# Wider VectorE operations, more raw slots, a third early granule pair and a spread residual in four feed-forward networks

## The chip, the core and the metric

One Trainium2 chip, one of its cores. The time is that of one execution of the whole program in device microseconds; the figure to compare is the median of several executions. One further execution was taken by the hardware profiler, and all rows below are from that one.

## What is computed

The input is 256 tokens of width 1024 and a conditioning vector c. A first block of two layers is followed by a second block of one layer with attention and a mixture of experts. Each of the two layers of the first block does, with nine columns sh, sc, g that are cut from `silu(c) @ w_ada[l] + b_ada[l]` (a vector of 9 x 1024):

```python
h = rmsnorm(x, norm_g[l, 0]) * (1 + sc1) + sh1
x = x + 0.5 * g1 * ((silu(h @ wg0) * (h @ wu0)) @ wd0)
h = rmsnorm(x, norm_g[l, 1]) * (1 + sc2) + sh2
x = x + g2 * mixer(h)            # l = 0: attention and pooling; l = 1: short convolution
h = rmsnorm(x, norm_g[l, 2]) * (1 + sc3) + sh3
x = x + 0.5 * g3 * ((silu(h @ wg1) * (h @ wu1)) @ wd1)
```

So there are four feed-forward networks, each 1024 to 2816 to 1024, all in float32. The change concerns these four, and what they share with the rest.

## The kernel before, in words

**Arithmetic.** Every float32 operand of a large product is split into a part that is rounded to the matmul's input format (ScalarE cast, line 227) and a remainder (VectorE subtraction, line 228). A product then is high x high + high x low + low x high. `mm2` (lines 238 to 243) does this with two matmuls: the weight's high part against both halves of the activation (512 columns), and the weight's low part against the high half (256 columns). `mm3`, and `pair` (lines 128 to 141), use three of 256 columns. Activations are held transposed: partition = feature, 256 tokens along the free dimension.

**A feed-forward network** is `ffn` (line 440). The 2816 inner features are eleven granules p = 0 to 10 of 256. For each granule one 1 MB tile of gate weights and one of up weights is loaded and split, two halves f of 128 features are accumulated in PSUM (f = 0: gate, up; f = 1: gate, up), and the result silu(gate) x up is split into an activation tile. Then comes the down projection in two halves h = 0, 1 of 512 output features. Each half runs over six pairs of granules (the last pair has one granule), with one 1 MB weight tile per pair; four accumulators live through the half, and after it the residual is added (line 526), squares are summed for the next norm, and the next norm's operand is built (`gap_chunk`, line 97).

**Granules that do not need h.** The norm's scale per token is known late. In the second to fourth network, granules 0 and 1 therefore multiply the weights with the merely scaled x (`aH`, `aL` in the tile xa); scale per token and shift are applied to the result (`gap_pair`, line 104; `gap_fin`, line 143). During granule 1 the eight chunks of the true h are built by GpSimd, ScalarE and VectorE (`h_chunk`, line 405, last step line 417), and granules 2 to 10 use h. In the first network granule 0 runs on h while the first columns are still being computed (`first_cols`), and granules 1 to 10 follow.

**Columns of w_ada.** 15 of the 18 column vectors are computed beside the networks and mixers. `gemv_steps` (line 295) is a generator; each step loads one 1 MB tile and does two VectorE operations of 1024 columns on the accumulator gacc (lines 305 and 307); each fourth step ends with eight small matmuls that sum over partitions (line 312), and the step after it with two transposes (line 271). `ffn` calls these steps from `advance` (line 448): in granules 2 to 10 and after each pair of the first half of the down projection, 13 places for the 16 steps of four columns. What is left is drained after the first half, where the gate column is needed.

**Buffers.** Loads go through SP's queue in program order (line 193). They take raw slots in a rotation (`set_ring`, `slot`, lines 168 to 178): in the networks three, raw twice and rawx. Split weights have three slots: two of "w" and the tile mix. PSUM has eight banks: four single-bank tiles `acc`, three `gu`, one `mi`.

**Second block.** `block2` (line 908) begins by building its own scaled operand hH, hL from x; `moe` runs the experts, whose weights are fetched early into any idle tile.

Of the kernel before, what the change touches and what calls it, by code (L numbers as in the profile page):

```python
# [44 lines left out]
class K:  # L45
    def __init__(self, tc, A, out, dbg=None):
        self.tc, self.nc, self.A, self.out, self.dbg = tc, tc.nc, A, out, dbg or {}
        self.last_dma = self.mark = None
        self.ring = self.wring = None
        self.pre = []  # L50
# [5 lines left out]
    def build(self):  # L56
        with ExitStack() as ctx:
# [9 lines left out]
            self.pacc = e(tc.tile_pool(name="pacc", bufs=4, space=PSUM))  # L67
# [36 lines left out]
    def gap_pair(self, src0, src1, n):  # L104
# [52 lines left out]

    def acc(self):
        return self.pacc.tile([P, 512], F32, tag="acc", name="acc")
# [8 lines left out]
    def set_ring(self, raw, wsp):  # L168

        if raw != self.ring:  # L170
            self.ring, self.ri = raw, 0
        if wsp != self.wring:
            self.wring, self.wi = wsp, 0

    def slot(self):
        kind = self.ring[self.ri % len(self.ring)]
        self.ri += 1
        return self.tile8(kind, "raw")
# [34 lines left out]
    def split(self, src, nk, n):  # L213

        r = self.load(src, nk * n)
        kind = self.wring[self.wi % len(self.wring)]
# [6 lines left out]
        self.wi += 1  # L223
        w = nk * n
        for lo in range(0, w, 1024):
            c = slice(lo, min(lo + 1024, w))
# [213 lines left out]
    def ffn(self, l, j, n, steps, count, done, ready=None):  # L440
# [4 lines left out]
        points = iter([4 * count * (i + 1) // 13 - 4 * count * i // 13 for i in range(13)])  # L445
        parts = []

# [4 lines left out]
        for p in range(NF):  # L452
# [8 lines left out]
            gap = p < 2 and not ready  # L461
            if gap:
                pss = self.gap_pair(g, u, n)
            elif p == 0:
                pss = self.pair(g, u, *n["h"], T, lambda k: [ready(i) for i in {0: (0, 1, 2), 2: (3,)}.get(k, ())])
                self.set_ring(self.ring[:NRAW + 1], self.wring)
            else:
                h2 = self.h2
                w = self.split(g, 8, T), self.split(u, 8, T)
            for f in range(2):  # L470
                a = self.t1()
                if gap:
                    s = self.t1()
                    tg, cg = self.gap_fin(n, pss[f])
                    nc.scalar.activation(s, tg, AF.Silu, bias=cg[:, 0:1])
                    tu, cu = self.gap_fin(n, pss[2 + f])
                    nc.vector.scalar_tensor_tensor(a, tu, cu[:, 0:1], s, op0=ALU.add, op1=ALU.mult)
                elif p == 0:
                    s = self.t1()
                    nc.scalar.activation(s, pss[f][:, :T], AF.Silu)  # L480
                    nc.vector.tensor_tensor(a, s, pss[2 + f][:, :T], op=ALU.mult)
                else:
                    c = slice(f * P, f * P + P)
                    gu = self.t2()
# [7 lines left out]
                    s = gu[:, :T]  # L492
                    nc.scalar.activation(s, s, AF.Silu)
                    nc.vector.tensor_tensor(a, s, gu[:, T:], op=ALU.mult)
                d = self.split_act(a, a4[:, f, :], a4[:, 2 + f, :])
                if p == 0:
                    self.mark = d
            if p >= 2:
                advance()
        stat, nxt = [], None  # L500
        pairs = [(p, min(p + 2, NF)) for p in range(0, NF, 2)]
        for h in range(2):
# [19 lines left out]
            for d in range(4):  # L522
                k = 4 * h + d
                x = self.xT[:, k, :]
                for z in range(2):
                    nc.vector.scalar_tensor_tensor(x, accs[d][:, z * T:z * T + T], hg[:, k:k + 1], x, op0=ALU.mult, op1=ALU.add)
                if d % 2:
                    self.sq_add(self.xT[:, k - 1:k + 1, :].rearrange("p a b -> p (a b)"), stat)
                if nxt is not None:
                    self.gap_chunk(nxt, k)  # L530
# [377 lines left out]
    def block2(self, stat):  # L908
        nc, A = self.nc, self.A
        hH, hL = self.h_tiles()  # L910
        o = VEC["attn_norm"][0]
        for k in range(8):
            g = self.vec[:, o + k:o + k + 1]
            nc.scalar.activation(hH[:, k, :], self.xT[:, k, :], AF.Copy, scale=g)
# [739 lines left out]
```

## Time and profile before

| | us |
|---|---|
| median of 3 runs | 1475.55 |
| lowest, highest | 1472.15, 1477.84 |
| the profiled execution | 1475.21 |
| its span, first to last instruction | 1473.4 |

By the matmuls' lines in the timeline the networks run from 22.0 to 231.4, 341.4 to 541.5, 541.5 to 741.0 and 843.8 to 1036.5 us (down projections from 161.5, 473.5, 672.4 and 972.6). Mixer and output projection of layer 0 lie between the first two, those of layer 1 between the last two; block 2 follows, and the experts take the rest from about 1245 us on. How to read the rows: an engine's busy time is the time in which it executed instructions; matmuls overlap, so a busy TensorE is not one at its peak, but an idle one is one that waits. "<-" behind an idle time names what ended it. The granted clock is a share of TensorE's full clock, 2.4 GHz; 0.50 is its lower level, 1.2 GHz.

### The profile page before, as it was taken

How to read it: one execution, taken by the hardware profiler on the slowest of the kernel's cores; microseconds unless marked ns; L12 is line 12 of the kernel's file. 1: busy time of each engine (PE TensorE's matmuls, PEld its weight loads, DVE VectorE, ACT ScalarE, POOL GpSimd, SP SyncE). 2: the span in 40 equal slices, each digit the busy share in tenths (PEclk: the TensorE clock that was granted, in tenths of full speed). 3: DMA queues.
4: the chain of work that ended last, by engine and by line, in shares of the span. 5: the costliest groups of instructions: out<-in, count | busy, mean ns of one | idle time of the engine just before them, and what ended most of it. 6: DMA issues, size and time to landing. Idle time of an engine off the chain costs nothing. (4 is left out here: it accounts for less than half of the span.)

```text
span 1473.4 us, 24454 instructions
## 1 busy us (share of the span) xinstructions
PE 1386.4 (94%) x9948; PEld 1152.6 (78%) x9949; DVE 962.4 (65%) x1650; ACT 688.3 (47%) x1202; POOL 79.5 (5%) x100
## 2 busy tenths in 40 slices
PE   6999999999999999999999999999999999997775
PEld 3888889879888788887889988888987999554332
DVE  4788777667998859988676687764767565211101
ACT  3555355546655436653544556544447655211011
POOL 0000002111000002000020020000121000000001
PEclk9999999999999999999999999999999999999797
DMA  8778774464787864878737446666434467999996
GB/s 337 264 284 296 285 279 151 155 245 175 256 292 285 286 229 176 308 288 300 269 148 276 151 158 225 230 224 236 172 133 174 144 257 302 376 420 421 420 419 281
DMA packets 70999, 380.35 MB, mean 258 GB/s; under 512 B 6624, under 2 KB 7136, under 8 KB 30944
## 3 DMA queue, kind: packets, MB, share of 16 engines
q1 hardware_dynamic: 70880, 378.72, 68.4%
q8 instruction: 81, 1.33, 0.3%
q14 instruction: 38, 0.31, 0.1%
HBM read 377.64 MB, written 1.05 MB: 257 GB/s over the span
## 5 line engine op out<-in xcount | busy, mean ns | idle before, releaser
L228 DVE TENSOR_TENSOR wl<-raw,wh 128x1024 fp32r<-128x1024 f32 (+1 forms) x282 | 343.0, 1226 | 88.6 <-ACT wh L227 88.0
L227 ACT CAST wh<-raw 128x1024 fp32r<-128x1024 f32 (+1 forms) x282 | 289.4, 1042 | 194.6 <-DMA raw<-in_ffn_wd_dram 50.3
L242 PE MATMUL acc<-h,wh 128*128 128x512 f32 x784 | 279.7, 399 | 4.7 <-DVE h L417 4.7
L243 PE MATMUL acc<-h,wl 128*128 128x256 f32 x784 | 219.9, 280 | 0.1
L242 PEld LDWEIGHTS acc<-h,wh 128*128 128x128 f32 x784 | 147.5, 188 | 43.1 <-DVE h L417 6.3
L243 PEld LDWEIGHTS acc<-h,wl 128*128 128x128 f32 x784 | 148.5, 189 | 0.6 <-DVE wl L228 0.4
L242 PE MATMUL acc<-h,wx 128*128 128x512 f32 x400 | 144.5, 400 | 2.2 <-DVE h L417 2.2
L228 DVE TENSOR_TENSOR wx<-raw,wx 128x1024 fp32r<-128x1024 f32 x99 | 121.7, 1240 | 29.6 <-ACT wx L227 29.3
L227 ACT CAST wx<-raw 128x1024 fp32r<-128x1024 f32 x99 | 102.0, 1048 | 63.5 <-PE acc L243 29.4
L307 DVE SCALAR_TENSOR_TENSOR gacc<-raw,cpad,gacc 128x1024 f32<-128x1024 f32 x91 | 116.6, 1281 | 15.3 <-DMA raw<-in_w_ada_dram 14.7
L236 PE MATMUL gu<-h,wl 128*128 128x256 f32 (+1 forms) x392 | 111.3, 284 | 1.9 <-DVE wl L228 1.7
L234 PE MATMUL gu<-h,wh 128*128 128x256 f32 (+1 forms) x392 | 112.3, 287 | 0.2 <-ACT t L895 0.2
L243 PE MATMUL acc<-h,wx 128*128 128x256 f32 x400 | 112.3, 281 | 0.0
L235 PE MATMUL gu<-h,wh 128*128 128x256 f32 (+1 forms) x392 | 111.0, 283 | 0.0
L242 PEld LDWEIGHTS acc<-h,wx 128*128 128x128 f32 x400 | 75.9, 190 | 20.7 <-DVE h L417 3.2
L242 PE MATMUL acc<-m,wh 128*128 128x512 f32 x248 | 88.6, 395 | 0.6 <-ACT wh L227 0.6
L490 ACT COPY t<-acc 128x256 f32<-128x256 f32 x148 | 54.5, 368 | 56.5 <-PE acc L243 55.2
L234 PEld LDWEIGHTS gu<-h,wh 128*128 128x128 f32 (+1 forms) x392 | 74.4, 190 | 3.6 <-ACT wh L227 0.8
L236 PEld LDWEIGHTS gu<-h,wl 128*128 128x128 f32 (+1 forms) x392 | 74.4, 190 | 3.4 <-DVE wl L228 2.5
L243 PEld LDWEIGHTS acc<-h,wx 128*128 128x128 f32 x400 | 76.1, 190 | 0.2
L1348 PE MATMUL gu<-ex,pp 128*32 128x256 f32 x928 | 59.6, 398 | 17.2 <-DMA ex<-in_w_exp_up_dram 8.5
L235 PEld LDWEIGHTS gu<-h,wh 128*128 128x128 f32 (+1 forms) x392 | 74.4, 190 | 0.0
(432 smaller groups left out, 2957.1 us busy)
## 6 DMA issues: line engine op xcount, KB each, us to landing
raw<-in_w_ada_dram SPq DMA_DIRECT2D x72, 1024.0 KB, 6.5
raw<-in_ffn_wg_dram SPq DMA_DIRECT2D x44, 1024.0 KB, 4.8
raw<-in_ffn_wu_dram SPq DMA_DIRECT2D x44, 1024.0 KB, 4.8
raw<-in_ffn_wd_dram SPq DMA_DIRECT2D x88, 512.0 KB, 5.8
ex<-in_w_exp_gate_dram SPq DMA_DIRECT2D x30, 1024.0 KB, 19.8
ex<-in_w_exp_up_dram SPq DMA_DIRECT2D x28, 1024.0 KB, 19.8
ex<-in_w_exp_down_dram SPq DMA_DIRECT2D x28, 1024.0 KB, 19.8
raw<-in_w_in_dram SPq DMA_DIRECT2D x18, 1024.0 KB, 4.8
```

Source lines behind the costliest of these rows:

```text
L227: self.nc.scalar.copy(wh[:, c], r[:, c])
L228: self.nc.vector.tensor_tensor(wl[:, c], r[:, c], wh[:, c].bitcast(F32), op=ALU.subtract)
L234: mm(out, wh, xh, start=start, stop=False, skip_group_check=True)
L235: mm(out, wh, xl, start=False, stop=False, skip_group_check=True)
L236: mm(out, wl, xh, start=False, stop=stop, skip_group_check=True)
L242: mm(out.rearrange("p (z t) -> p z t", z=2), wh, x2, start=start, stop=False, skip_group_check=True)
L243: mm(out[:, :T], wl, x2[:, 0], start=False, stop=stop, skip_group_check=True)
L307: d = nc.vector.scalar_tensor_tensor(acc, g[:, kk, :], c, acc, op0=ALU.mult, op1=ALU.add)
L490: nc.scalar.copy(y, ps[:, T:])
L1348: nc.tensor.matmul(ps[32 * e:32 * e + 32, z * T:z * T + T], xg[:, k * P + 32 * e:k * P + 32 * e + 32], w[:, e, kk, :], start=(k == 0), sto ...
```

## The change

- `acc` tiles become two tiles of two banks (`acc2`); `acc()` hands out their halves. In the granules on h, gate and up of one f share a tile, and copy and addition out of PSUM handle both at once.
- `split_act` is called once per granule with 512 columns instead of twice with 256.
- `self.cut`: from granule 2 (granule 3 where 0 to 2 run ahead of h) to the network's end, casts and subtractions of a weight tile go over 2048 columns at once instead of 1024. Otherwise 1024 stays.
- Granule 2 of the second to fourth network runs ahead of h as well; the eight h chunks are spread over granules 1 and 2, four each.
- `spare`: the two halves of xa become raw slots from granule 3 on (granule 1 in the first network) to the end of gate/up, the two halves of h during the down projection, except in the last network. Slots and split-weight tiles are chosen by least recent use (`oldest`) instead of in rotation.
- `advance` has 21 places: granules 2 to 10, and after each pair of both halves. Four columns get one step per granule, then 1, 0, 1, 0, 1, 0 and 0, 1, 0, 1, 0, 1; the single column of the last network gets 1, 0, 1, 0. At the gate, `made` runs as many steps as the columns needed there ask for (one, by the count), and the rest is drained at the network's end.
- Residual: after the first half, two of its four accumulators are added at once and two behind the first matmuls of the second half; squares and next operand (`after`) of the first four chunks follow after steps 1 to 4 of the second half. The second half takes the short pair fourth instead of first.
- The last network builds block 2's operand as its "next norm's operand" (`last`), so `block2` no longer does.

```diff
     def gap_pair(self, src0, src1, n, parts=1):
-        n["h"] = self.h_tiles()
+        if "h" not in n:
+            n["h"], n["todo"] = self.h_tiles(), iter(range(8))
         def chunk(k):
-            self.h_chunk(k, n["h"], n["rb"], n["a"], n["b"], True)
+            k = next(n["todo"]) if k % parts == 0 else None
+            if k is not None:
+                self.h_chunk(k, n["h"], n["rb"], n["a"], n["b"], True)
+    def spare(self, kind):
+        t = self.two(kind, F32, "raw")
+        self.turns[(kind + "0", 0)] = self.turns[(kind + "1", 0)] = self.turn
+        return [(kind + str(z), t[:, z, :2048]) for z in range(2)]
+    def oldest(self, kinds):
+        seen, best = {}, None
+        for k in kinds:
+            q = k if isinstance(k, str) else k[0]
+            n = seen[q] = seen.get(q, -1) + 1
+            t = self.turns.get((q, n), -1)
+            if best is None or t < best[0]:
+                best = t, (q, n), k
+        self.turns[best[1]] = self.turn = self.turn + 1
+        return best[2]
     def split(self, src, nk, n):
-        for lo in range(0, w, 1024):
-            c = slice(lo, min(lo + 1024, w))
+        for lo in range(0, w, self.cut):
+            c = slice(lo, min(lo + self.cut, w))
     def ffn(self, l, j, n, steps, count, done, ready=None):
-        points = iter([4 * count * (i + 1) // 13 - 4 * count * i // 13 for i in range(13)])
+        points = iter([1] * 9 + [1, 0] * 3 + [0, 1] * 3 if count > 1 else [1, 0] * 7)
...
-            gap = p < 2 and not ready
+            gap = p < 3 and not ready
...
+                first = p == (1 if ready else 3)
+                if first:
+                    self.set_ring(ring + self.spare("xa"), self.wring)
+                if p >= 2:
+                    self.cut = 2048
                 w = self.split(g, 8, T), self.split(u, 8, T)
+                for f in range(2):
+                    ps = self.acc2()
                     c = slice(f * P, f * P + P)
                     for z, (wh, wl) in enumerate(w):
-                        ps = self.acc()
                         for k in range(8):
-                            self.mm2(ps, wh[:, k, c], wl[:, k, c], h2[:, :, k, :], start=(k == 0), stop=(k == 7))
-                        y = gu[:, z * T:z * T + T]
-                        nc.scalar.copy(y, ps[:, T:])
-                        nc.vector.tensor_tensor(y, y, ps[:, :T], op=ALU.add)
+                            self.mm2(ps[:, z], wh[:, k, c], wl[:, k, c], self.h2[:, :, k, :], start=(k == 0), stop=(k == 7))
+                    y = self.t2().rearrange("p (z t) -> p z t", z=2)
+                    nc.scalar.copy(y, ps[:, :, T:])
+                    nc.vector.tensor_tensor(y, y, ps[:, :, :T], op=ALU.add)
...
-                d = self.split_act(a, a4[:, f, :], a4[:, 2 + f, :])
+            d = self.split_act(a2, a4[:, 0:2, :], a4[:, 2:4, :])
...
+        if l == j == 1:
+            self.set_ring(ring, self.wring)
+        else:
+            self.set_ring(ring + self.spare("h"), self.wring)
         for h in range(2):
-            todo = pairs if h == 0 else pairs[-1:] + pairs[:-1]
+            todo = pairs if h == 0 else pairs[:3] + pairs[-1:] + pairs[3:-1]
...
-                if h == 0:
-                    advance()
+                    if late:
+                        residual(*late.pop(0))
+                if h == 1 and 0 < i < 5:
+                    after(i - 1)
+                advance()
             if h == 0:
-                for _ in steps:
-                    pass
                 gate, nxt = done()
...
+                residual(0, accs[0])
+                residual(1, accs[1])
+                late += [(2, accs[2]), (3, accs[3])]
+            else:
+                for _ in steps:
+                    pass
+                for d in range(4):
+                    residual(4 + d, accs[d])
+                    after(4 + d)
+        self.cut = 1024
+        self.set_ring(ring, self.wring)
```

## Rows read from the trace of the kernel before

**Rows 1.** The page's busy time, share of the span and instructions, by engine.

```profile
PE 1386.4 (94%) x9948; PEld 1152.6 (78%) x9949; DVE 962.4 (65%) x1650; ACT 688.3 (47%) x1202; POOL 79.5 (5%) x100
```

**Rows 2.** Stretches: length, busy of five engines, clock, DMA share, GB/s.

```profile
core 0: us, PE busy (x) PEld busy (x) DVE busy (x) ACT busy (x) POOL busy (x), PEclk, DMA share, GB/s
48.00:161.50 113.50, 113.50 (x655) 97.37 (x654) 99.61 (x146) 64.38 (x118) 0.00 (x0) 1.00 0.76 276
...
366.30:473.50 107.20, 104.62 (x598) 89.80 (x597) 97.84 (x152) 61.86 (x116) 3.13 (x3) 0.98 0.77 277
...
672.40:741.00 68.60, 65.25 (x379) 54.87 (x377) 49.89 (x62) 28.90 (x34) 0.10 (x1) 1.00 0.78 275
...
972.60:1036.50 63.90, 63.90 (x377) 54.76 (x375) 36.40 (x48) 25.20 (x32) 0.61 (x1) 1.00 0.61 223
```

**Rows 3.** TensorE's waits in 40:210, then 362:1020: us, times, longest.

```profile
PE gu L312 <- DVE gacc L307: 1.8, 1, 1.8
PE acc L243 <- DVE wl L228: 0.8, 1, 0.8
PE acc L242 <- ACT wh L227: 0.6, 1, 0.6
...
PE acc L242 <- DVE h L417: 6.9, 6, 2.1
PE gu L312 <- DVE gacc L307: 3.9, 2, 2.1
...
PE gu L243 <- DVE wl L228: 1.0, 1, 1.0
PE acc L243 <- DVE wl L228: 0.3, 1, 0.3
```

**Rows 4.** Two stretches of lower granted clock, same columns as rows 2.

```profile
370.80:374.20 3.40, 3.40 (x13) 2.70 (x12) 3.40 (x8) 2.53 (x4) 0.00 (x0) 0.50 0.30 58
500.50:503.90 3.40, 3.40 (x12) 2.90 (x11) 2.41 (x3) 1.38 (x2) 0.00 (x0) 0.50 0.64 224
```

**Rows 5.** TensorE's timeline: start us, us, instruction; granule 1, then one on h.

```profile
354.84 0.28 PE L138 MATMUL gu<-xa,wx 128*128 128x258 f32 x1
...
366.28 0.39 PE L242 MATMUL acc<-h,wh 128*128 128x512 f32 x1
...
450.57 0.50 PE L242 MATMUL acc<-h,wh 128*128 128x512 f32 x1
...
461.99 0.38 PE L271 MATMUL gu<-cst,gev 128*128 128x128 f32 x2
```

**Rows 6.** VectorE's timeline, end of a first half of down projection.

```profile
493.66 2.61 DVE L307 SCALAR_TENSOR_TENSOR gacc<-raw,cpad,gacc 128x1024 f32<-128x1024 f32 x2 [1.29 <-DMA raw<-in_w_ada_dram]
496.48 2.61 DVE L307 SCALAR_TENSOR_TENSOR gacc<-raw,cpad,gacc 128x1024 f32<-128x1024 f32 x2 [0.21 <-DMA raw<-in_w_ada_dram]
```

**Rows 7.** The page's DMA issues: down-projection tile, median us to landing.

```profile
raw<-in_ffn_wd_dram SPq DMA_DIRECT2D x88, 512.0 KB, 5.8
```

**Rows 8.** Timelines of VectorE and ScalarE: two subtractions, two casts in a row.

```profile
344.97 2.35 DVE L228 TENSOR_TENSOR wx<-raw,wx 128x1024 fp32r<-128x1024 f32 x2
...
359.00 1.98 ACT L227 CAST wh<-raw 128x1024 fp32r<-128x1024 f32 x2
```

**Rows 9.** VectorE's groups by form: 512-wide subtraction, busy us, mean ns.

```profile
L228 DVE TENSOR_TENSOR wl<-raw,wh 128x512 fp32r<-128x512 f32 x3 | 2.1, 684 | 0.0
```

**Rows 10.** Timelines of ScalarE, VectorE, TensorE: one up tile.

```profile
436.82 1.06 ACT L227 CAST wx<-raw 128x1024 fp32r<-128x1024 f32 x1
...
437.90 1.22 DVE L228 TENSOR_TENSOR wx<-raw,wx 128x1024 fp32r<-128x1024 f32 x1 [0.50 <-ACT wx L227]
439.05 1.28 DVE L307 SCALAR_TENSOR_TENSOR gacc<-raw,cpad,gacc 128x1024 f32<-128x1024 f32 x1
...
440.57 1.22 DVE L228 TENSOR_TENSOR wx<-raw,wx 128x1024 fp32r<-128x1024 f32 x1
...
441.59 0.39 PE L242 MATMUL acc<-h,wx 128*128 128x512 f32 x1
```

More of the change, by code (lines that the diff above doesn't have):

```diff
@@ L66, in build @@
             self.sp = e(tc.tile_pool(name="sp", bufs=3))
-            self.pacc = e(tc.tile_pool(name="pacc", bufs=4, space=PSUM))
+            self.pacc = e(tc.tile_pool(name="pacc", bufs=2, space=PSUM))
             self.pgu = e(tc.tile_pool(name="pgu", bufs=3, space=PSUM))
@@ L156, in small, with acc2 @@
         return self.sp.tile([P, w], dt, tag=f"{tag}{w}", name=f"sm{w}")
+    def acc2(self):
+        self.acc_rest = None
+        return self.pacc.tile([P, 2, 512], F32, tag="acc", name="acc")
     def acc(self):
-        return self.pacc.tile([P, 512], F32, tag="acc", name="acc")
+        if self.acc_rest is not None:
+            t, self.acc_rest = self.acc_rest, None
+            return t
+        t = self.acc2()
+        self.acc_rest = t[:, 1]
+        return t[:, 0]
     def gu(self):
@@ L498, in ffn, with residual @@
+                    nc.vector.tensor_tensor(y, y, ps[:, :, :T], op=ALU.add)
+                    nc.scalar.activation(y[:, 0], y[:, 0], AF.Silu)
+                    nc.vector.tensor_tensor(a2[:, f], y[:, 0], y[:, 1], op=ALU.mult)
+            d = self.split_act(a2, a4[:, 0:2, :], a4[:, 2:4, :])
+            if p == 0:
+                self.mark = d
             if p >= 2:
                 advance()
-        stat, nxt = [], None
+        stat, nxt, late = [], None, []
         pairs = [(p, min(p + 2, NF)) for p in range(0, NF, 2)]
+        def residual(k, ps):
+            x = self.xT[:, k, :]
+            for z in range(2):
+                nc.vector.scalar_tensor_tensor(x, ps[:, z * T:z * T + T], hg[:, k:k + 1], x, op0=ALU.mult, op1=ALU.add)
@@ L502, in ffn, with after @@
+        def after(k):
+            if nxt is not None:
+                self.gap_chunk(nxt, k)
+            if k % 2:
+                self.sq_add(self.xT[:, k - 1:k + 1, :].rearrange("p a b -> p (a b)"), stat)
+        if l == j == 1:
+            self.set_ring(ring, self.wring)
+        else:
+            self.set_ring(ring + self.spare("h"), self.wring)
         for h in range(2):
             accs = [self.acc() if h == 0 or d > 1 else self.gu() for d in range(4)]
-            todo = pairs if h == 0 else pairs[-1:] + pairs[:-1]
+            todo = pairs if h == 0 else pairs[:3] + pairs[-1:] + pairs[3:-1]
@@ L521, in ffn @@
                 nc.vector.tensor_scalar(hg, gate, 0.5, None, op0=ALU.mult)
[L522 to L530, printed above, removed]
+                residual(0, accs[0])
+                residual(1, accs[1])
+                late += [(2, accs[2]), (3, accs[3])]
+            else:
+                for _ in steps:
[3 more added lines that the diff above has]
+                    after(4 + d)
+        self.cut = 1024
+        self.set_ring(ring, self.wring)
         if nxt is None:
@@ L905, in attend, with block2 @@
         yield
-    def block2(self, stat):
+    def block2(self, stat, h):
         nc, A = self.nc, self.A
[L910 to L914, printed above, removed]
-            nc.vector.scalar_tensor_tensor(hL[:, k, :], self.xT[:, k, :], g, hH[:, k, :].bitcast(F32), op0=ALU.mult, op1=ALU.subtract)
+        hH, hL = h
         rope = self.slot()
@@ L1289, in moe @@
         ng = VEC["ffn_norm"][0]
+        self.acc_rest = None
         accs = [self.acc() for _ in range(4)]
@@ L1498, in body, with last, made @@
                 [(1, 3), (1, 4), (1, 5), (1, 6)], [], [(1, 8)]]
+        def last():
+            aH, aL = self.h_tiles()
+            return {"a": self.v("attn_norm"), "aH": aH, "aL": aL}
         begin = lambda l, i: self.gap_begin(self.scale_col(l, i, m[(l, 3 * i + 1)]), m[(l, 3 * i)])
+        def made(g, keys):
+            while not all(k in m for k in keys):
+                next(g, None)
+            return m[keys[0]]
         n = {"h": h}
         for l in range(2):
-            n = self.ffn(l, 0, n, steps(*plan[3 * l]), len(plan[3 * l]), lambda: (m[(l, 2)], begin(l, 1)), ready if l == 0 else None)
+            g = steps(*plan[3 * l])
+            n = self.ffn(l, 0, n, g, len(plan[3 * l]), lambda: (made(g, [(l, 2), (l, 3), (l, 4)]), begin(l, 1)), ready if l == 0 else None)
             self.debug(f"x{l}a", self.xT)
@@ L1512, in body @@
             self.set_ring(raws, ffn_ring[1])
-            n = self.ffn(l, 1, n, steps(*plan[3 * l + 2]), len(plan[3 * l + 2]),
-                         lambda: (m[(l, 8)], None if l else begin(1, 0)))
+            g = steps(*plan[3 * l + 2])
+            n = self.ffn(l, 1, n, g, len(plan[3 * l + 2]),
+                         lambda: (made(g, [(l, 8)] + [(1, 0), (1, 1)] * (1 - l)), last() if l else begin(1, 0)))
             self.debug(f"x{l}c", self.xT)
```

60 lines of the change are left out of this document (23 added, 37 removed).

## The prediction, made before the change was run

> **What bounds the kernel now.** I read the page's busy shares first: TensorE is busy 94% of the span, VectorE 65% [rows 1]. A share of the whole span says nothing of a stage, so the busy time by stretch comes next. In the first network's granules on h (48 to 161.5 us) TensorE has no idle time at all while VectorE is busy 99.6 of 113.5 us; in the second network's it idles 2.6 of 107.2 us with VectorE at 97.8; in the third network's down projection 3.4 of 68.6, in the last network's nothing [rows 2]. So TensorE sets the pace of all four networks, VectorE is a close second, and an edit can only give back time in which TensorE waits. Third, the chain of TensorE's waits over those stretches names them [rows 3]: 6.9 us (six waits) for the h chunks, when a network's third granule begins; 1.8 + 3.9 us for the last sums of an adaptive-modulation column (gacc) at the end of the first half of a down projection; 0.8 + 0.6 + 1.0 + 0.3 us for split weight tiles of the down projection. Together 15.3 us. Fourth, the granted clock: after two of the gacc waits and two of the h waits TensorE shows 3.4 us at 0.50, the lower of its two levels, of which two stand in [rows 4]; the other two, at 189.9 and 872.6, are the same length. Half speed for 3.4 us loses 1.7 us, four times 6.8. All that the change can remove in the networks is so 15.3 + 6.8 = 22.1 us.
>
> The sum is made against the profiled execution, 1475.21 us (span 1473.4, 1.8 around it); the median of the runs shown is 1475.55, so the result needs no shift. A measurement of this kernel can tell about 0.5%, 7.4 us, from no change.
>
> **Third granule pair ahead of h.** Granule 2 of the second, third and fourth network no longer reads h but the scaled x, as granules 0 and 1 do. Its 96 matmuls take as long as the 64 they replace: from the first matmul of such a pair to the next granule 354.84 to 366.28, 11.44 us; a granule on h 450.57 to 461.99, 11.42 us [rows 5]. Cost 0.02 us, three times: nothing. The eight h chunks have two granules instead of one, and are needed 11.4 us later than now; the worst wait now is 2.1 us [rows 3]. I take all six h waits away and their two clock drops: -6.9 - 3.4 = -10.3 us. What is late next is granule 3's split weights, which share VectorE with the chunks; I put 0.5 us per network against that, +1.5.
>
> **Gemv steps spread over both halves.** Now 16 steps go into 13 places, the last two into one, ending inside the first half of the down projection; afterwards there is one per granule, three in the first half, one forced where the gate is needed, three in the second half. The row to see is VectorE's gacc pair at 493.66, which waited 1.29 us for its weights to land, and the next at 496.48, 0.21 us [rows 6]: the first half fetches a weight tile and a modulation tile per step. With three steps instead of five the last of the first half is not queued behind a transfer. I take the three waits away with two clock drops: -(1.8 + 3.9) - 3.4 = -9.1 us. The forced step puts two transposes of the finished column and two VectorE operations on a new raw tile at the point where residual and next norm begin; they queue on VectorE ahead of the residual. Bounds: 0 and the present 2.1 us each time; I take 0.5, three times, +1.5, since half a tile of TensorE work (2.8 us) lies before it.
>
> **More raw slots.** Two more in gate/up (in the idle xa) and two in the down projection (in h). The transfers on SP's queue go up to five tiles ahead instead of three, so the split waits at the start of the down projections should go: -0.8 - 0.6 - 1.0 - 0.3 = -2.7. The first h slot cannot be filled before the last gate/up matmul, and SP's queue waits there with what is behind it; two tiles, 11.4 us of matmuls, are then still ahead of TensorE, against 5.8 us median landing [rows 7] and 4.3 us of split (below). That fits with 1.3 us to spare.
>
> **Wider operations.** A pair of 1024-wide subtractions takes 2.35 us, a pair of casts 1.98 [rows 8]. A 512-wide subtraction takes 0.684 us [rows 9], a 1024-wide one 1.22 [rows 10], so 1024 columns more cost 2 x 0.536 = 1.07 and a 2048-wide one some 2.29 us: 0.06 less than the pair. With two subtractions, two additions out of PSUM and one activation split merged, VectorE saves about 5 x 0.06 = 0.3 us per granule. TensorE's matmuls hide all of it; if VectorE were the bound it would be worth 33 granules x 0.3 = 10 us. On the other side whole tiles come later. One "up" tile shows it [rows 10]: cast at 436.82, first half subtracted at 437.90, second only at 440.57 to 441.79, because a gacc operation (1.28 us) went between; TensorE takes the tile from 441.59, beginning with the half that was done at 439.12. As one piece the cast ends near 438.8, the subtraction runs 439.2 to 441.5 behind one gacc operation, which is just in time, and behind two it ends at 442.7, 1.1 us late. Bounds per granule 0 and 1.1 us; I take 0.1, near the lower end, because deeper prefetch lets gacc operations run earlier and there is one step per granule instead of 1.2: 33 x 0.1 = +3.3 us.
>
> The Trainium skill speaks against this edit: "Perfetto Trace Analysis", section "Optimizing Scalar/DVE Operations", says that where these engines are not saturated but leave bubbles on another, smaller instructions let work finish sooner, and grouping helps when they are saturated. By it the sum would go towards the 1.1 us end. At 97.8 of 107.2 us [rows 2] the trace has VectorE almost saturated, and shows no bubble from a split tile in the gate/up stretches.
>
> **Residual spread, two-bank accumulators, block 2's operand built ahead.** The evacuation of gate and up waits for both, but the other two-bank tile takes 5.7 us of matmuls (half a granule) meanwhile; the evacuation is two copies, an addition and a product, each under 0.7 us by the 512-wide row [rows 9]: 0. Two of the four residuals of the first half move behind the next step's matmuls; TensorE's waits show none for the residual. The last network's end has no idle time now [rows 2], so the earlier operand gains 0.
>
> Sum: -10.3 - 9.1 - 2.7 + 1.5 + 1.5 + 3.3 = -15.8, and 1475.2 - 15.8 = **1459.4 us**. Bounds: all 22.1 gone and nothing new, 1453; the additions at twice their size, 1466.
>
> **Rivals.**
> Partly given back: the waits come back smaller, the h chunks behind granule 3's splits, the gacc sum at the end of the second half, or 0.3 us per granule. Against it stands that TensorE is served without a wait in the first network now; for it, VectorE's 91% in the second. If half the gain returns, 1475.2 - 8 = 1467; with 0.4 us per granule (13 us), 1469; up to 1475.
>
> Late whole tiles, slower: one mechanism, in every granule with 2048-wide splits. The "up" tile's slot is freed when gate's last matmul is through, a quarter of a granule before its end, and the tile is needed a quarter into the next, 5.7 us in all; cast and subtraction take 4.3. One gacc operation of 1.28 in front uses that up, two exceed it by 1.1 us. At 33 granules x 1.1 = 36 us against 19 of other gain the time is 1475.2 + 17 = 1493; it decides from 19 / 33 = 0.57 us per granule on, and a longer wait also brings the lower clock. This is the case which the page's rule above describes.
>
> The change doesn't do what it says: the two spare slots are halves of one tile, and if a fill of one half waits for the readers of the other, or the least-recently-used choice picks a slot that is still held (the first weight tile after an output projection now goes to the tile that its operand sits in), the extra slots bring nothing. Then the 2.7 and part of the 9.1 stay: 1466 to 1470.
>
> **How the numbers follow.** Forecast 0.57, partly given back 0.22, slower by late tiles 0.14, slots without effect 0.07. The bound for faster is 1468.2, for slower 1482.9. Forecast and a third of the two middle rivals lie below: 0.57 + 0.11 = 0.68. Within 0.5%: 0.18. Slower: 0.14. The range of the likeliest case is 1453 to 1466; to leave out no more than 2 in 10 it reaches to 1476, which takes in the middle rivals, and down to 1452.
>
> **What would show it.** Right: no TensorE wait for h chunks and none of over 1 us before the gacc sums; granted clock 1.00 all through the networks; networks two to four each 3 to 6 us shorter; VectorE's busy time lower by about 10 us. Wrong: TensorE waits for the subtraction (wl, wx) in the middle of gate/up, as many as there are granules; waits for h moved to granule 3; a gacc wait at the end of the second half; a mixer, block 2 or the expert stage longer by more than 2 us.

## The result and the profile after

The changed kernel takes 1468.44 us, the median of 10 runs (1465.0 to 1472.13); the kernel before took 1477.03 us beside it, also in 10 runs. The ratio is 0.9937, with a 95% interval of 0.9921 to 0.9953: 9.3 us less by the ratio (8.6 between the medians), where 15.8 were forecast. The profiled execution took 1472.13 us, the longest of the ten, with a span of 1470.3. A second profile of the same kernel (the first experiment) has a span of 1466.5.

Each profile is cut where TensorE's timeline changes from one kind of matmul to the next: the first `mm2` on h, the first matmul on the scaled x behind an output projection, the first on an expert's weights. "Three edits" is the kernel with three edits together, near the end of the experiments.

| stretch, us | before | changed | changed, second profile | three edits |
|---|---|---|---|---|
| start to the first `mm2` on h | 44.9 | 46.4 | 48.8 | 47.5 |
| four networks, with the two output projections | 827.8 | 812.7 | 811.2 | 804.5 |
| two mixers | 163.8 | 163.6 | 161.2 | 161.3 |
| block 2, up to the first expert matmul | 224.6 | 230.0 | 230.4 | 226.1 |
| experts | 212.3 | 217.7 | 214.9 | 213.1 |
| of it, last expert weight landed to end | 13.7 | 18.6 | 15.6 | 13.7 |
| span | 1473.4 | 1470.3 | 1466.5 | 1452.5 |

So the networks gave 15.1 and 16.6 us, what was forecast for the whole. Behind them 5.4 to 5.8 us were lost in block 2 and 2 to 5 at the end of the experts.

The page's busy time by engine, which answers to [rows 1]: VectorE is busy 21.6 us less in 206 fewer instructions, where the prediction named some 10 us.

```profile
PE 1382.7 (94%) x10044; PEld 1155.7 (79%) x10045; DVE 940.8 (64%) x1444; ACT 663.7 (45%) x972; POOL 78.1 (5%) x100
```

The chain of waits of TensorE in two windows, 40 to 210 us and 362 to 1020 us, answers to [rows 3] (TensorE's wait, what for, us in total, times, longest; the shortest left out):

```profile
PE acc L272 <- DVE wl L257: 1.1, 2, 0.6
PE acc L272 <- DVE wx L257: 0.2, 1, 0.2
...
PE gu L263 <- ACT wx L256: 1.5, 1, 1.5
PE mi L390 <- ACT sq L381: 1.0, 1, 1.0
PE gu L143 <- ACT wx L256: 0.7, 1, 0.7
PE acc L272 <- DVE wl L257: 0.5, 1, 0.5
```

No wait for h and none for gacc is left. The busy time by stretch of the second network's granules on h, its down projection and the last network's down projection (columns as in [rows 2]) shows TensorE 0.5, 0.3 and 0 us short of the stretch, at full clock:

```profile
377.56:469.75 92.19, 91.65 (x534) 79.05 (x533) 80.67 (x89) 50.09 (x56) 0.00 (x0) 1.00 0.71 277
469.75:534.95 65.20, 64.94 (x378) 54.83 (x376) 50.56 (x54) 27.23 (x26) 0.00 (x0) 1.00 0.83 308
...
960.15:1022.70 62.55, 62.55 (x364) 54.20 (x362) 31.41 (x33) 24.00 (x22) 1.07 (x1) 1.00 0.55 194
```

What is new stands at the edges. TensorE's timeline where the second network begins, then ScalarE's: the output projection ends at 338.95; the first gate tile is named wx, which is the tile mix, and its cast starts only at 341.26, behind the work on x.

```profile
338.95 1.06 PE L390 MATMUL mi<-sq,ones 128*32 128x256 f32 x12
341.01 0.63 PE L390 MATMUL mi<-sq,ones 128*32 128x256 f32 x4 [1.00 <-ACT sq L381]
342.34 0.39 PE L143 MATMUL gu<-xa,wx 128*128 128x258 f32 x1 [0.71 <-ACT wx L256]
...
341.26 1.98 ACT L256 CAST wx<-raw 128x1024 fp32r<-128x1024 f32 x2
```

Before, the first matmul on the scaled x came 0.5 us behind the output projection, on a tile named wh:

```profile
340.84 0.62 PE L361 MATMUL mi<-sq,ones 128*32 128x256 f32 x4
341.39 0.39 PE L138 MATMUL gu<-xa,wh 128*128 128x258 f32 x1
```

Now it comes 3.4 us behind it, in the second and in the fourth network. Behind the second of these waits the granted clock falls to its lower level, the one such stretch in the networks (before there were four); busy time by stretch:

```profile
833.30:836.70 3.40, 3.40 (x18) 3.40 (x17) 3.02 (x3) 1.39 (x2) 0.00 (x0) 0.50 0.20 24
```

TensorE's waits in block 2 of the changed kernel:

```profile
PE gu L1360 <- DVE t L1352: 1.5, 1, 1.5
PE mi L390 <- ACT sq L381: 1.3, 1, 1.3
PE gu L265 <- DVE wl L257: 1.0, 2, 0.8
PE mi L404 <- DVE t L398: 1.0, 1, 1.0
PE acc L265 <- DVE wl L257: 0.7, 1, 0.7
PE acc L264 <- DVE m L452: 0.6, 1, 0.6
```

The last two, at block 2's output projection, and the wait for a square are not in the profile before, though of block 2's code only the building of its operand was moved. To see where block 2 loses, cut it at its first transpose of `pp` (the attention weights) and at the first matmul on `selb` (the choice of experts), in TensorE's timeline before and in the second profile of the changed kernel:

```profile
1112.01 0.49 PE L893 MATMUL gu<-cst,pp 128*128 128x128 f32 x3
1257.33 0.29 PE L1255 MATMUL mi<-selb,bt 128*128 128x32 bf16 x5 [0.28 <-DVE selb L1251]
...
1099.68 0.49 PE L948 MATMUL gu<-cst,pp 128*128 128x128 f32 x3
1247.82 0.29 PE L1305 MATMUL mi<-selb,bt 128*128 128x32 bf16 x5 [0.16 <-DVE selb L1301]
```

From block 2's start to the first of these points it takes 75.5 us before and 78.1 and 78.5 in the changed kernel's two profiles; between the points 145.3 before, and 148.1 in both.

### The profile page after: what moved, and what is told of

The parts are those of the page before. It is cut to its first block, busy times and chain, and to the rows that moved or that the text cites. A ratio compares the mean times of both kernels' runs of the same rounds, so it can differ in the third digit from the quotient of the medians.

```text
span 1470.3 us, 24174 instructions
## 1 busy us (share of the span) xinstructions
PE 1382.7 (94%) x10044; PEld 1155.7 (79%) x10045; DVE 940.8 (64%) x1444; ACT 663.7 (45%) x972; POOL 78.1 (5%) x100
## 5 line engine op out<-in xcount | busy, mean ns | idle before, releaser
L257 DVE TENSOR_TENSOR wl<-raw,wh 128x1024 fp32r<-128x1024 f32 (+1 forms) x208 | 324.8, 1571 | 108.4 <-ACT wh L256 106.8
L256 ACT CAST wh<-raw 128x1024 fp32r<-128x1024 f32 (+1 forms) x208 | 272.6, 1325 | 210.8 <-PE acc L271 56.3
L271 PE MATMUL acc<-h,wh 128*128 128x512 f32 x704 | 248.9, 395 | 0.0
L272 PE MATMUL acc<-h,wl 128*128 128x256 f32 x704 | 197.7, 281 | 1.1 <-DVE wl L257 1.1
L271 PEld LDWEIGHTS acc<-h,wh 128*128 128x128 f32 x704 | 131.9, 187 | 31.6 <-issue 1.2
L257 DVE TENSOR_TENSOR wx<-raw,wx 128x2048 fp32r<-128x2048 f32 (+1 forms) x67 | 121.9, 1824 | 30.9 <-ACT wx L256 30.9
L256 ACT CAST wx<-raw 128x2048 fp32r<-128x2048 f32 (+1 forms) x67 | 101.1, 1519 | 55.8 <-PE acc L272 36.2
L263 PE MATMUL gu<-h,wh 128*128 128x256 f32 (+1 forms) x344 | 98.2, 285 | 0.2 <-ACT t L950 0.2
L264 PE MATMUL gu<-h,wh 128*128 128x256 f32 (+1 forms) x344 | 97.5, 283 | 0.1
L272 PE MATMUL acc<-m,wl 128*128 128x256 f32 x272 | 77.0, 283 | 0.7 <-DVE wl L257 0.6
L263 PEld LDWEIGHTS gu<-h,wh 128*128 128x128 f32 (+1 forms) x344 | 65.2, 190 | 2.4 <-ACT t L950 0.5
L264 PEld LDWEIGHTS gu<-h,wh 128*128 128x128 f32 (+1 forms) x344 | 65.2, 190 | 0.3 <-DVE h L103 0.3
```

The source lines that it names most:

```text
L256: self.nc.scalar.copy(wh[:, c], r[:, c])
L257: self.nc.vector.tensor_tensor(wl[:, c], r[:, c], wh[:, c].bitcast(F32), op=ALU.subtract)
L263: mm(out, wh, xh, start=start, stop=False, skip_group_check=True)
L264: mm(out, wh, xl, start=False, stop=False, skip_group_check=True)
L271: mm(out.rearrange("p (z t) -> p z t", z=2), wh, x2, start=start, stop=False, skip_group_check=True)
L272: mm(out[:, :T], wl, x2[:, 0], start=False, stop=stop, skip_group_check=True)
```

## The experiments

All twelve start from the changed kernel. "Networks" below is the second line of the table, 811.2 us in the second profile; times are medians of 5 or 6 runs (12 for three of them, 7 for one), ratios are against the kernel before beside them. The intervals are 0.2 to 0.3% wide to either side, some 4 us, so what is smaller is read from the stretches, one profile each.

**Once more.** No edit.

> The changed kernel once more, for a second profile and more times. Theory: the profiled execution of the changed kernel lost 1.9 us before its first matmul (first matmul at 9.43 instead of 7.53 us) and 4.9 us behind its last expert weight (last landing to end 18.6 instead of 13.7 us), and both are luck of that execution; then a second profile shows network stages within 0.5 us of the first, one or both of these two within 1 us of the kernel before, and a median of 1467 to 1470. Rival: they belong to the change; then both stand again as before and the span is again within 4 us of the kernel before.

1469.63 us, ratio 0.9929 (0.9903 to 0.9956). Network stretches agree with the first profile within 0.7 us, but for the gap granules (those ahead of h) of the last network (35.2 against 36.7: the lower clock above). The end went from 18.6 to 15.6 us, not to 13.7: part of it is luck, 2 us are not. The first matmul again came at 9.5 us, but at 7.5 to 9.5 over all profiles, whatever the edit, and at 7.5 and 7.6 in two of the kernels below: that is no effect of the change.

**mix counted as most recently used** before networks two and four.

```diff
             self.set_ring(raws, ffn_ring[1])
+            self.turns[("mix", 0)] = self.turn = self.turn + 1
```

> Before the second network of each layer the tile mix counts as the most recently used split slot, so that the first gate tile no longer takes it. Theory (the least-recent choice gives the first gate tile the slot that the output projection's operand sits in): the time from the squares behind the output projection to the first matmul of networks two and four falls from 3.4 to 0.5 us each, and the half-clock stretch at 833 us goes: 2 x 2.9 + 1.7 = 7.5 us less than the changed kernel, some 1461 us. Rival (the wait comes from the residual, squares and scaled operand that queue on ScalarE and VectorE there): it stays at 3 us or more, and the time within 2 us of the changed kernel.

1466.76 us, 0.9914 (0.9885 to 0.9942). TensorE's timeline at the same place:

```profile
336.27 0.63 PE L390 MATMUL mi<-sq,ones 128*32 128x256 f32 x4
336.82 0.39 PE L143 MATMUL gu<-xa,wh 128*128 128x258 f32 x1
```

The tile is wh again and the 3.4 us are 0.5: the cause is the choice of slot. Its worth was less than the 7.5 us expected: the squares that filled part of the 3.4 us now stand 1.2 us inside the network (gap granules 36.4 instead of 35.2 us), so output projection and gap granules together get 1.8 and 1.6 us shorter. Block 2 lost 2.3 us, with a wait of 2.2 us for a split there whose cast had waited 2.18 us for its weights to land; why they came late was not settled.

**Block 2 builds its own operand** (the lines of the diff that moved it are taken back).

```diff
-        hH, hL = h
+        hH, hL = self.h_tiles()
...
-lambda: (made(...), last() if l else begin(1, 0))
+lambda: (made(...), None if l else begin(1, 0))
```

> The last network does not build block 2's operand; block 2 does, as in the kernel before. Theory (casts and products of the operand stand ahead of the last squares on ScalarE, which shows as 1.4 us of TensorE waiting for a square): the wait for the square goes and the start of block 2, to the end of its first projections, is 2 to 3 us shorter than in the changed kernel: about 1466 us. Rival (the later start only moves the work): block 2 ends at the same distance from the last network's end, and the time stays within 1 us.

1467.24 us, 0.9908 (0.9882 to 0.9935). The wait for a square went, but block 2 took 229.7 instead of 230.4 us. In this profile half-clock stretches of 3.4 us begin at 1028.7, 1083.3 and 1250.6, the last at block 2's end; the second profile has none there. Each can cost up to 1.7 us, so the worth of the edit can't be read from this profile; the last run below comes back to it.

**Single-bank accumulators everywhere.**

```diff
-self.pacc = e(tc.tile_pool(name="pacc", bufs=2, space=PSUM))
+self.pacc = e(tc.tile_pool(name="pacc", bufs=4, space=PSUM))
...
-nc.scalar.copy(y, ps[:, :, T:])
-nc.vector.tensor_tensor(y, y, ps[:, :, :T], op=ALU.add)
+nc.scalar.copy(y[:, z], ps[:, T:])
+nc.vector.tensor_tensor(y[:, z], y[:, z], ps[:, :T], op=ALU.add)
```

> Single-bank accumulators as in the kernel before, gate and up copied and added out of PSUM one by one; all else as changed. Theory (halves of a two-bank tile wait for each other's readers in block 2, seen as 0.7 and 0.8 us at the output projection): block 2 gets 1 to 2.5 us shorter, the networks stay within 0.5 us each, VectorE's busy time rises by some 5 us: about 1467 us. Rival (VectorE is so near the bound that the merged evacuation is what keeps TensorE fed): networks two and three lose over 1 us each.

1466.86 us, 0.9908 (0.9883 to 0.9934). Both theories hold, each in its place: block 2 falls from 230.4 to 228.9 us, though a half-clock stretch stands at its start (1026.6), and the granules on h of networks two to four get 1.5, 0.6 and 2.2 us longer. The waits in the second network, from its granules on h to its end:

```profile
PE acc L261 <- DVE wl L246: 2.0, 1, 2.0
PE acc L261 <- DVE wx L246: 0.8, 1, 0.8
```

So the merged evacuation is worth some 4 us in these granules, and the two-bank tile costs something behind the networks. The first network got 2.3 us shorter instead, so that all four with their output projections are only 1.0 us longer; why was not sought.

**Two granules ahead of h.**

```diff
-            gap = p < 3 and not ready
+            gap = p < 2 and not ready
...
-                    pss = self.gap_pair(g, u, n, 2)
+                    pss = self.gap_pair(g, u, n)
...
-                first = p == (1 if ready else 3)
+                first = p == (1 if ready else 2)
```

The spare slots in xa and the wide splits so begin a granule earlier too.

> The changed kernel with two granules ahead of h instead of three, all eight h chunks in the second of them, as in the kernel before. Theory (the third granule took away the h waits): at granule 2 of networks two, three and four TensorE waits twice for h, some 2 us each, with a half-clock stretch behind it in two of them: the three networks together 8 to 10 us longer than with three (573.6 us in the second profile of the changed kernel), the time 1477 to 1480. Rival (fewer VectorE instructions and deeper slots already bring the h chunks in time): waits for h below 0.5 us, the three networks within 2 us, the time 1468 to 1471.

1482.08 us, ratio 1.0022 (1.0000 to 1.0044): 13.7 us more than the changed kernel by the ratios. Networks two to four take 586.4 us, 12.8 more than in the second profile and 10.9 more than in the first. TensorE's waits in network two and three, then in four:

```profile
PE acc L271 <- DVE h L446: 5.7, 6, 2.2
...
PE acc L271 <- DVE h L446: 2.5, 2, 2.2
```

They are the waits of [rows 3], with three half-clock stretches behind them (370.5, 568.5 and 868.9). Taking the third granule away costs all of its forecast 10.3 us and a little more.

**Column steps where they were.**

```diff
-points = iter([1] * 9 + [1, 0] * 3 + [0, 1] * 3 if count > 1 else [1, 0] * 7)
+points = iter([4 * count * (i + 1) // 13 - 4 * count * i // 13 for i in range(13)])
...
+                for _ in steps:
+                    pass
                 gate, nxt = done()
```

> The changed kernel with the column steps where the kernel before had them: 16 in 13 places that end in the first half of the down projection, the rest drained ahead of the gate. Theory (fewer steps in the first half took away the gacc waits): TensorE waits 1.8 to 2.1 us for gacc at the end of the first half in networks one, two and three, with a half-clock stretch behind two of them: the three down projections together 6 to 9 us longer than 195 us, the time 1475 to 1479. Rival (the two slots more in the down projection bring the column's weights in time, whatever the places): waits below 0.5 us, the time within 2 us of the changed kernel.

1487.53 us, 1.0051 (1.0029 to 1.0073), 18 us more than the changed kernel. The first three down projections take 207.6 instead of 195.0 us. But the wait is another one; that of the second network's:

```profile
PE acc L272 <- DVE wl L257: 2.2, 1, 2.2
PE gu L300 <- DVE gev L344: 0.5, 1, 0.5
PE acc L271 <- DVE t L526: 0.5, 1, 0.5
```

VectorE's timeline shows four gacc operations in a row in front of it, none of them waiting for its weights, then a wait for the column's sum, and the split that TensorE needs only behind that:

```profile
492.54 5.24 DVE L336 SCALAR_TENSOR_TENSOR gacc<-raw,cpad,gacc 128x1024 f32<-128x1024 f32 x4
499.56 0.43 DVE L344 COPY gev<-gu 128x256 f32<-128x256 f32 x1 [1.77 <-PE gu L341]
...
500.82 2.29 DVE L257 TENSOR_TENSOR wl<-raw,wh 128x2048 fp32r<-128x2048 f32 x1
```

With the deeper ring the column's weights are in time, and the drained steps hold up the splits on VectorE instead of being late themselves. That the last network and block 2 lost 7 us as well was not followed up.

**Splits of 1024 columns everywhere.**

```diff
-                    self.cut = 2048
+                    self.cut = 1024
```

> The changed kernel with casts and subtractions of 1024 columns everywhere; all else as changed. Theory of the prediction (whole tiles come later, 0.1 us for each of 33 granules): the networks get some 3 us shorter, VectorE's busy time 5 to 7 us longer, the time about 1465. Rival one (whole tiles are in time and the merged operations only relieve an engine that is not the bound): networks within 1 us in sum, the time within 1 us. Rival two (the relief is what keeps TensorE fed): TensorE waits for splits in granules of h, networks together 2 us longer or more.

1465.28 us, 0.9898 (0.9867 to 0.9930). Networks 806.8 us: 4.4 less than with 2048. VectorE is busy 949.8 us, 9.2 more, and of TensorE's waits for a split in the networks two are left, of 0.6 and 0.3 us. The second network's down projection, busy time by stretch, against 64.94 of 65.20 above:

```profile
465.47:529.47 64.00, 64.00 (x377) 54.76 (x375) 50.99 (x63) 28.87 (x36) 0.00 (x0) 1.00 0.86 319
```

The first three down projections take 191.7 us here and 193.1 to 195.2 in the five profiles with 2048 columns and nothing else undone in them (the changed kernel's two, the edits to mix and to block 2's operand, and that to the banks below). Some 2.5 us of the price stand in the down projections, 0.8 in the granules on h.

**Without the slots in xa and h.**

```diff
-                    self.set_ring(ring + self.spare("xa"), self.wring)
+                    self.set_ring(ring, self.wring)
...
-            self.set_ring(ring + self.spare("h"), self.wring)
+            self.set_ring(ring, self.wring)
```

> The changed kernel without the raw slots in xa and h: three raw slots as before, chosen by least recent use. Theory (the slots hide the transfers at the start of the down projections and the column weights): TensorE waits 0.5 to 1 us for splits at the start of each down projection and the gacc sums come up to 1 us late: networks one to three together 3 to 6 us longer, the time 1471 to 1475. Rival (three slots do as soon as one step comes per granule): within 1 us.

1478.87 us, 1.0004 (0.9981 to 1.0027). Networks 821.0 us, 9.8 more; waits of 0.8 to 1.0 us for split tiles and for VectorE's t (what it takes out of PSUM) stand in the first two networks, at six places. Three slots do not do, at one step per granule either.

**Single-bank tiles from block 2 on.** The two-bank pool is closed where block 2 begins, and `acc` then takes one-bank tiles of a new pool; the networks stay as changed.

```diff
-            self.body()
+            with tc.tile_pool(name="pacc", bufs=2, space=PSUM) as self.pacc:
+                stat = self.body()
+            self.single = True
+            self.pacc = e(tc.tile_pool(name="pacc1", bufs=4, space=PSUM))
+            self.rest(*stat)
...
     def acc(self):
+        if self.single:
+            return self.pacc.tile([P, 512], F32, tag="acc", name="acc")
```

> The changed kernel, but the four accumulator banks become single-bank tiles where block 2 begins; the networks keep the two-bank tiles. Theory (a half of a two-bank tile is not free, and not readable, until the other half is done): block 2 holds its distance to the kernel before from its second quarter on (2 to 3 us less than changed), the last additions of the experts overlap the last matmuls again (last landing to end 13.7 to 14.5 us at full clock instead of 15.6), networks as changed: 4 us less, about 1465. Rival (the delays in block 2 come from other work, or giving the banks over costs a wait of its own): block 2 within 1 us of changed.

1463.33 us, 0.9883 (0.9858 to 0.9907). Block 2 takes 226.5 instead of 230.4 us; its waits for m and for wl at the output projection are gone, though two half-clock stretches stand in it (1081.6 and 1245.4). The two points in it:

```profile
1097.52 0.49 PE L954 MATMUL gu<-cst,pp 128*128 128x128 f32 x3
1242.62 0.29 PE L1311 MATMUL mi<-selb,bt 128*128 128x32 bf16 x5 [0.15 <-DVE selb L1307]
```

Between them lie 145.1 us. In all nine profiles with two-bank tiles there it is 148.1 to 148.2, in all five with single banks 145.0 to 145.3, whatever else was edited: the two-bank tiles cost 3.0 us in block 2. The part in front of the first point, 75.5 us before, takes 76.4 to 82.5 with two-bank tiles and 76.8 to 80.0 with single ones; so what it lost can't be put down to the tiles, and its cause was not found. The end of the experts took 15.2 us here, not the 13.7 to 14.5 expected: a half-clock stretch from 1446.8 on holds the first of the last matmuls.

**Residual as it was,** the short pair first in the second half.

```diff
-            todo = pairs if h == 0 else pairs[:3] + pairs[-1:] + pairs[3:-1]
+            todo = pairs if h == 0 else pairs[-1:] + pairs[:-1]
...
-                if h == 1 and 0 < i < 5:
-                    after(i - 1)
...
-                residual(0, accs[0])
-                residual(1, accs[1])
-                late += [(2, accs[2]), (3, accs[3])]
+                for d in range(4):
+                    residual(d, accs[d])
+                    after(d)
```

> The changed kernel with the residual, squares and next operand of the first half all directly behind it and the short pair first in the second half, as in the kernel before. Theory of the prediction (the spread is worth nothing, since TensorE showed no wait for it): networks within 1 us in sum, the time within 2 us of the changed kernel. Rival (without the fewer operations in front of the second half's first split, TensorE waits for splits there, or the banks of the second half come free late): 1 us or more per down projection, the time 1471 to 1476.

1472.79 us, 0.9951 (0.9924 to 0.9979). The first three down projections take 200.3 us, 5.3 more, 1.1 to 2.5 each; the order of the pairs and the place of the residual were not undone apart. TensorE waits 0.7 us for xT in the first two, and in the second for a split as well:

```profile
PE acc L271 <- DVE xT L540: 0.7, 1, 0.7
PE acc L272 <- DVE wx L257: 0.7, 1, 0.7
```

**Three edits together:** narrow splits, mix as most recently used, single banks from block 2 on.

> Three edits together: splits of 1024 columns everywhere, mix as most recently used slot before networks two and four of the order, single-bank accumulators from block 2 on. If they add, 4 + 6 + 4 = 14 us less than the changed kernel's 1469: 1455, with transitions of 0.5 us, networks of 752 us in sum and no TensorE wait over 0.7 us in them. If block 2's first weight tiles, which have two raw slots, eat part of it, as they seem to do with mix alone (2.4 us of waiting for a split there), 1458 to 1460.

1456.03 us, 0.9831 (0.9805 to 0.9857): 13.6 us below the changed kernel's second median (14.5 by the ratios), the sum of 14 that was expected of the three. The last matmuls and the additions behind them, from the timelines of the changed kernel's second profile, then of this kernel:

```profile
1451.86 3.70 PE L1432 MATMUL acc<-t,t 128*128 128x512 f32 x8
1454.74 2.48 DVE L1440 TENSOR_TENSOR a<-acc,a 128x512 f32<-128x512 f32 x4 [7.02 <-PE acc L1432]
```

```profile
1439.78 3.70 PE L1438 MATMUL acc<-t,t 128*128 128x512 f32 x8
1440.94 0.69 DVE L1446 TENSOR_TENSOR a<-acc,a 128x512 f32<-128x512 f32 x1 [4.42 <-PE acc L1438]
1441.80 0.69 DVE L1446 TENSOR_TENSOR a<-acc,a 128x512 f32<-128x512 f32 x1 [0.17 <-PE acc L1438]
...
```

With single banks the first addition starts 1.2 us after the last eight matmuls began, in step with them; with two-bank tiles it starts 2.9 us after. The code accumulates in the order 0, 2, 1, 3, and accumulators 0 and 1 are the halves of one two-bank tile: the addition on 0 starts when 1, the third of the four, is through. That makes the 2 us at the end. In the five profiles with two-bank tiles and 3.70 us of last matmuls the program ends 14.60 us after they began, in the four such with single banks 12.7.

**And block 2 builds its own operand.**

> As the kernel with three edits, and block 2 builds its operand itself. Theory (squares come earlier in the last network's end): 1 to 2 us less than without. Rival (the later operand only shifts the work behind the squares): within 1 us or slower.

1454.34 us, 0.9826 (0.9802 to 0.9850). The median is 1.7 us lower than with three edits, as the theory had it, but the ratios differ by 0.7 us only, and both lie within the intervals. Block 2 is 1.3 us longer, but two half-clock stretches stand in it (1017.7 and 1236.1) that the profile with three edits lacks; the span is 0.3 shorter. Which of the two is right stays open; what hangs on the place is less than these runs tell apart.

## Why the prediction was right, and where its sum was off

**What bounds the kernel** was right: TensorE in the networks, and only its waits could be given back. Without the wide splits the networks and output projections give 827.8 - 806.8 = 21.0 us.

**Third granule:** forecast 10.3, undoing it costs 10.9 to 12.8. Right, down to the clock: the waits come back at the same places with a half-clock stretch behind each network's.

**Steps over both halves:** forecast 9.1, undoing it costs 12.6 in the three down projections. The direction was right; that the column's transfer was the cause holds at most for the old ring. Once the transfers run ahead, the drained steps crowd out splits. The 1.5 us put against the forced step did not show: no wait at the gate, in neither profile of the changed kernel.

**Slots:** forecast 2.7, undoing them costs 9.8. The step counted only waits for splits. That the other parts need the slots as well was missed: these sums of undoing (12.8, 12.6, 9.8 and 5.3 for the residual, less 4.4 for the wide splits: 36) are more than twice the networks' gain of 16.6, so the parts cover in part the same waits, which return if any of them is missing.

**Wide splits:** forecast a loss of 3.3, measured 4.4. The size was about right, the place was not: it was worked out on an up tile in 33 granules, and most of it stands in the down projections, where the same edit merges 40 more splits that the sum had no term for. There a step of two gacc operations (2.60 us in VectorE's timeline) goes between two splits, which may be why; it was not tried apart. The relief of VectorE was sized too low as well: 21.6 us instead of 10, for 206 instructions instead of 165 and at 0.10 us each instead of 0.06; TensorE hid it, as the prediction said. The Trainium skill ("Perfetto Trace Analysis", "Optimizing Scalar/DVE Operations") says that smaller instructions may let work finish sooner where VectorE is not saturated but causes bubbles on other engines. This case agrees in sign: VectorE is busy 80.67 of 92.19 us in the second network's granules on h, and the smaller splits are 4.4 us faster. The 36 us rival made of it does not hold.

**Edits costed at nothing** are the step that failed. "The evacuation of gate and up waits for both [...]: 0" looked for the price of the two-bank tile in the networks alone. `acc` hands the halves of that tile to block 2 and the experts too, and there a half waits for the other one: 3.0 us in block 2 and 1.9 at the end, shown by the runs with single banks from block 2 on. At the end the trace shows the mechanism itself; in block 2 only its price is shown. "The last network's end has no idle time now [rows 2], so the earlier operand gains 0": no run tells it from 0. "TensorE's waits show none for the residual", so 0, was wrong by 5 us in the other direction. That in the kernel before the drained steps and the gacc waits stood at the same place and hid it fits, but was not tried.

**The rival "doesn't do what it says"** had named that the first weight tile after an output projection now goes to the tile that the operand sits in. That happened in both places, and cost 3.4 us net of the squares that moved into the wait, and up to 1.7 more by the clock. It belonged in the sum: it followed from the code and not from luck.

The networks' part came out at 15.1 and 16.6 against 15.8 because misses of both signs cancelled, which is luck. The whole fell short by what stands behind them: 5 us of the two-bank tiles, and 2.6 to 3.0 at the start of block 2 whose cause is open. So one sign of "wrong" came true, block 2 longer by more than 2 us, beside signs of "right": no wait for h or gacc, and full clock in the networks but for one stretch in one profile. The second network got 4.2 us shorter with its output projection, the third 6.5 (6.3 in the second profile) and the fourth 0.2 to 1.8, where 3 to 6 each were named as the sign; the first got 4.2 shorter. Two slips in the prediction's sums change nothing: a third of the two middle rivals is 0.10, not 0.11, and 1475.2 + 17 is 1492, not 1493.

## What to carry to other kernels

When a shared helper changes what it hands out, price it at every caller, also in stages that the change is not about: here the granules of three networks gained some 4 us by two-bank accumulators (all four networks 1.0) and the stages behind them lost 5, and other tiles from there on kept the gain without the loss. A least-recently-used choice needs to be told of uses that don't pass through it, such as an operand that sits in a weight slot. Undo each part on its own afterwards: one part of a change that gained was a loss of 4 us, and three small edits more than doubled the gain.

## What was not expected

The end of the experts is a matter of clock as well: the last eight accumulating matmuls (128x512) took 3.70 us in the second profile of the changed kernel and 5.80 in the first, where they fell into a half-clock stretch, and the time from the last expert weight to the end ranged from 13.7 to 18.7 us over 14 profiles of 13 kernels. The two profiles of the changed kernel differ by 3.9 us in span: by 2.8 in the experts, by 2.4 in the mixers and 1.5 in the networks, where half-clock stretches stand in the first alone (307.6 for 6.9 us, and 833.3), and by 2.4 the other way at the start. That is more than some of the edits are worth: a single profile's span would have shown a gain of 3.1 us here, where the ratio of the medians shows 9.3. How much of the spread between unprofiled runs is the clock's, no run shows.
